# A spacer of 256 bytes between two generations of buffers in a hybrid decoder block

## The chip, the cores and the metric

The kernel is one launch on one core of a Trainium2 chip. The metric is the device time of that launch in microseconds (us). Of the kernel before, three timed runs are known (1938.85, 1940.31 and 1944.94 us; the median is 1940.31 us) and one profiled execution, whose trace is read here.

## The reference, cut to what matters

One layer of a decoder block, on a sequence of 2048 rows of width 1024, all in float32:

```
h = x + concat[RMSNorm(PoolMix(u)), RMSNorm(StickBreakAttn(q, k, v))] @ w_out
        with [u | q | k | v] = RMSNorm(x) @ w_in
up  = RMSNorm(h) @ w_up            # 1024 -> 4096
act = square(relu(up))
h   = h + act @ w_down             # 4096 -> 1024
y   = RMSNorm(h)
```

Only the last two products bear on this change. In the kernel the product with `w_up` is called layer one (function `up`) and the product with `w_down` layer two (function `down`).

## The kernel before, in words

Each float32 operand is split into two parts: a rounded copy that ScalarE writes (L146) and the remainder that VectorE writes (L147). A product is then three matmuls: high by high, high by low, low by high.

Both layers use Strassen's scheme: seven products P1 to P7 of half blocks, with sums made ahead on VectorE. Layer one runs over 16 columns of weights in two passes; each column is seven slots of 12 matmuls (L1052), accumulated in three PSUM banks named `pX`, `pY` and `pZ`. The split weights of a slot (`hw`) live in a ring of six buffers, the pool `hlp`. After a slot, `post` empties its bank: L987 copies it (`u`), L981 and L982 are relu and square, L997, L1005 and L1021 add a bank to an earlier copy, L1012, L1015, L1017 and L1025 form sums, L976 stores each result to DRAM (`sd`). For some results `inner_sums` makes more sums (L881, L883, L885, L887) and stores them (`sdi`, L879); its rows `hr` are read by L870. The last column's slots end with P7 and P4 (bank `pY`) and P3 (bank `pZ`). P3 goes on adding to the bank that L1005 reads first, and L1021 reads the finished P3.

Layer two starts with its product P1: eight steps `kk`, each of 48 matmuls (L1392), 24 for each half `q` of the rows. A step takes one block of weights (`wr`, loaded by L1121, 512 KB, split into `wd`), and two blocks of rows (`ar`, loaded by L1171 from layer one's results, 512 KB each, split into `ad`). It also takes a second weight block that L1125 subtracts from; the difference is stored (`td`, L1127). The rings are: `rt` with six buffers for `wr`, `rs` with five for `ar`, `t8` with three for `wd`, `s8` with five for `ad`. The residual rows `res` are read by L1196.

All these loads and stores are issued from SyncE's queue (SP), in order. Each uses one of eight semaphores in turn (DMAHW0 to DMAHW7), and waits until the transfer eight places ahead in the queue has landed.

Layer one's pools are closed before layer two's are opened, so the bytes are handed on. A buffer of layer two that shares even one byte with a buffer of layer one waits for the last reader of that buffer. The order of the instructions on each engine is not written by hand: a planner sets it when the kernel is built, from a model of when each instruction could run, and a wait of that kind goes into its model.

The pool `rs` begins where `pupa`, which holds 2 x 8192 bytes, ends: at byte 44,224 of each partition. Layer one's ring `hlp` ends at byte 44,288. The buffer of `hlp` that lies there, bytes 40,192 to 44,287, holds the split weights of layer one's very last slot, P3 of the last column.

Of the kernel before, what the change touches and what calls it, by code (L numbers as in the profile page):

```python
# [8 lines left out]
F32 = mybir.dt.float32  # L9
# [6 lines left out]
P = 128  # L16
# [24 lines left out]
DA = 2  # L41
# [5 lines left out]
def hymba_block(ctx: ExitStack, tc: tile.TileContext, xT, gains, w_in, pool_w, w_out, w_up, w_down, out):  # L47
# [1378 lines left out]
    def catch_up(n):  # L1426
        for _ in range(n):
            with ExitStack() as behind:
                for ins in (last_split[0], done[0]):
                    if ins:  # L1430
                        behind.enter_context(tc.issue_after(ins.ins))
                later.pop(0)()
# [42 lines left out]
    def ffn():  # L1475
        catch_up(len(later))
        front_scope.close()
        for _ in layer.pop():
            pass
        left_scope.close()  # L1480
        with ExitStack() as scope:
            spool = lambda name, bufs, **kw: scope.enter_context(tc.tile_pool(name=name, bufs=bufs, reuse_waits="tile", **kw))

            rlp, pupa, rs, rt, t8 = spool("rlp", 2), spool("pupa", 2), spool("rs", 5), spool("rt", 6), spool("t8", DA + 1)
            s8, tmp2, pup, rsp = spool("s8", 2 * DA + 1), spool("tmp2", 2), spool("pup", 6), spool("rsp", 2)
            down([t8, s8, rs, rt, pupa, pup, rsp, rlp, tmp2, spool("psb", 1, space=PS)])

# [21 lines left out]
    tail(True)  # L1509
    run()  # L1510
    ffn()


    count = P * H * (TB * NT - 2)
    got = nc.values_load(zeros[0:1, 0:1], min_val=0, max_val=count)
    with tc.If(got < count):
        wlist.clear(), raws.clear(), grans.clear(), gates.clear(), marks.clear()
        state["gran"], last_split[0], last_mm[0], done[:] = 0, None, None, (None, None)
        open_pools(front_scope)
        open_big(left_scope)  # L1520
        open_att(att_scope)
        for j in range(NT):
            far(j)
        att_scope.close()
        open_last(front_scope, last_scope)
        open_out(out_scope)
        tail(False)
        run()
        ffn()
# [44 lines left out]
```

## Time and profile before

| | us |
|---|---|
| median of the three runs | 1940.31 |
| the profiled execution's own time | 1938.94 |
| its span in the trace | 1937.1 |
| TensorE matmuls, busy | 1902.7 |
| VectorE, busy | 1383.2 |
| ScalarE, busy | 991.2 |

PE is TensorE's matmuls, PEld its weight loads, DVE is VectorE, ACT is ScalarE, POOL is GpSimd, SP is SyncE, and SPq is SyncE's queue that issues transfers. The granted clock (PEclk) is the share of its full speed at which TensorE was allowed to run. A row of the timeline gives a start, a length, the engine, the line, the operation with output and input, a count, and in brackets the idle time just before and what ended it.

### The profile page before, as it was taken

The numbers are of one execution on the slowest core, as the hardware profiler recorded it, in microseconds if no ns is written. First come the engines' busy times: TensorE is split into PE (matmuls) and PEld (weight loads), VectorE is DVE, ScalarE is ACT, GpSimd is POOL, SyncE is SP. The second block draws the span as 40 slices with busy tenths as digits, with TensorE's granted clock in tenths as the row PEclk, the third lists the DMA queues.
The fourth block names the chain that finished last, engine by engine and source line by source line (L and its number), as shares of the span: only waits on it lengthen the run. The fifth ranks groups of instructions, "written<-read, shape, count | busy, mean of one in ns | idle before, by whom it ended". The sixth has DMA issues, their size and how long they took to land.

```text
span 1937.1 us, 26281 instructions
## 1 busy us (share of the span) xinstructions
PE 1902.7 (98%) x9043; PEld 1588.3 (82%) x9043; DVE 1383.2 (71%) x2026; ACT 991.2 (51%) x1580; POOL 210.2 (11%) x399
## 2 busy tenths in 40 slices
PE   9999999999999999999999999997999999999997
PEld 7888888888888888888888888886888888887887
DVE  6887799668876975767587677774565558649874
ACT  5565566455544555555575555552333255425643
POOL 0211123102111110000000000000020020006120
PEclk9999999999999999999999999998999999999999
DMA  6686686888696964677476666579798869958852
GB/s 214 205 269 190 214 283 211 269 307 289 235 382 227 327 198 156 209 248 247 170 251 230 227 211 238 206 278 366 257 324 291 275 247 323 332 191 275 316 206 89
DMA packets 197359, 483.44 MB, mean 250 GB/s; under 512 B 22496, under 2 KB 42976, under 8 KB 193120
## 3 DMA queue, kind: packets, MB, share of 16 engines
q1 hardware_dynamic: 197072, 481.40, 72.2%
q8 instruction: 73, 1.20, 0.3%
q14 instruction: 70, 0.57, 0.1%
q10 hardware_dynamic: 144, 0.26, 0.0%
HBM read 320.10 MB, written 161.48 MB: 249 GB/s over the span
## 4 chain that ended last, share of the span: by engine, by line
PE 84%; issue 8%; DVE 4%; DMA 2%; POOL 1%; ACT 1%; SPq 0%; DVEq 0%; ACTq 0%; POOLq 0%
PE pY L1052 17%; PE pb L1392 17%; PE pZ L1052 8%; PE pd L175 8%; PE pd L177 8%; PE pd L176 8%; PE pX L1052 4%; PE pb L1230 2%; PE po L672 2%; PE pta L661 1%; PE pr L228 1%; PE pz L614 1%; PE pm L202 1%; DMA res<-hs 1%; PE pz L615 1%
## 5 line engine op out<-in xcount | busy, mean ns | idle before, releaser
L1392 PE MATMUL pb<-ad,wd 128*128 128x512 f32 x1872 | 429.8, 392 | 12.5 <-ACT ad L146 12.5
L1392 PEld LDWEIGHTS pb<-ad,wd 128*128 128x128 f32 x1872 | 352.9, 189 | 85.9 <-ACT ad L146 12.9
L1052 PE MATMUL pY<-sa,hw 128*128 128x512 f32 x1536 | 364.3, 390 | 1.2 <-ACT u L987 1.2
L1052 PEld LDWEIGHTS pY<-sa,hw 128*128 128x128 f32 x1536 | 288.2, 188 | 61.6 <-ACT u L987 2.0
L175 PE MATMUL pd<-h,hl 128*128 128x512 f32 x752 | 299.4, 398 | 0.7 <-DVE qkr L421 0.7
L177 PE MATMUL pd<-h,hl 128*128 128x512 f32 x752 | 296.6, 394 | 0.0
L176 PE MATMUL pd<-h,hl 128*128 128x512 f32 x752 | 296.5, 394 | 0.0
L146 ACT ACTIVATE ad<-ar 128x1024 fp32r<-128x1024 f32 x136 | 143.0, 1053 | 117.6 <-PE pb L1392 70.1
L147 DVE TENSOR_TENSOR ad<-ar,ad 128x1024 fp32r<-128x1024 f32 x136 | 175.2, 1298 | 32.6 <-ACT ad L146 32.5
L1052 PE MATMUL pZ<-sa,hw 128*128 128x512 f32 x768 | 184.7, 390 | 0.0
L1052 PEld LDWEIGHTS pZ<-sa,hw 128*128 128x128 f32 x768 | 144.2, 188 | 29.8
L175 PEld LDWEIGHTS pd<-h,hl 128*128 128x128 f32 x752 | 141.9, 189 | 28.0 <-DVE qkr L421 1.0
L177 PEld LDWEIGHTS pd<-h,hl 128*128 128x128 f32 x752 | 141.6, 188 | 27.7
L176 PEld LDWEIGHTS pd<-h,hl 128*128 128x128 f32 x752 | 141.7, 188 | 26.8
L146 ACT ACTIVATE hl<-raw 128x512 fp32r<-128x512 f32 x168 | 103.7, 630 | 108.2 <-PE pd L177 70.7
L1230 PE MATMUL pb<-ad,wd 128*128 128x512 f32 x672 | 153.9, 390 | 2.5 <-DVE ad L147 2.4
L1230 PEld LDWEIGHTS pb<-ad,wd 128*128 128x128 f32 x672 | 125.8, 188 | 30.3 <-DVE ad L147 4.4
L147 DVE TENSOR_TENSOR hl<-raw,hl 128x512 fp32r<-128x512 f32 x168 | 114.3, 687 | 49.4 <-ACT hl L146 48.9
L147 DVE TENSOR_TENSOR hw<-rt,hw 128x512 fp32r<-128x512 f32 x128 | 87.7, 688 | 56.8 <-ACT hw L146 55.9
L146 ACT ACTIVATE wd<-wr 128x1024 fp32r<-128x1024 f32 x48 | 50.7, 1061 | 148.7 <-PE pb L1392 126.5
L147 DVE TENSOR_TENSOR wd<-wr,wd 128x1024 fp32r<-128x1024 f32 x48 | 58.6, 1222 | 52.9 <-ACT wd L146 52.8
L1052 PE MATMUL pX<-sa,hw 128*128 128x512 f32 x384 | 93.1, 390 | 0.0
(213 smaller groups left out, 2632.2 us busy)
## 6 DMA issues: line engine op xcount, KB each, us to landing
ar<-sd SPq DMA_DIRECT2D x104, 512.0 KB, 5.7
rb<-in_w_up_dram SPq DMA_DIRECT2D x32, 1024.0 KB, 6.1
wr<-in_w_down_dram SPq DMA_DIRECT2D x64, 512.0 KB, 5.3
sd<-a SPq DMA_DIRECT2D x112, 256.0 KB, 3.3
raw<-in_w_in_dram SPq DMA_DIRECT2D x50, 512.0 KB, 4.9
sd<-s SPq DMA_DIRECT2D x96, 256.0 KB, 3.7
raw<-in_w_out_dram SPq DMA_DIRECT2D x32, 512.0 KB, 5.6
ar<-sdi SPq DMA_DIRECT2D x32, 512.0 KB, 5.5
```

What stands on the lines that cost most here:

```text
L146: nc.scalar.activation(hi, src, AF.Copy)
L147: return nc.vector.tensor_tensor(lo, src, hi.bitcast(F32), ALU.subtract)
L175: nc.tensor.matmul(ps, hl[:, 0, c], hi, start=(k == 0), stop=False)
L176: nc.tensor.matmul(ps, hl[:, 0, c], lo, start=False, stop=False)
L177: mm = nc.tensor.matmul(ps, hl[:, 1, c], hi, start=False, stop=(k == n - 1))
L202: marks["pm"] = nc.tensor.matmul(pm[:, c:c + 1], ss[:, c * P:(c + 1) * P], inv[n], start=(i == 0), stop=(i == len(parts) - 1))
L228: mm = nc.tensor.matmul(pr[:, b * P:(b + 1) * P], yr[:, x, b:b + 1].to_broadcast([P, P]), identr, start=(b == 0 and x == 0), stop=(b == TB ...
L614: nc.tensor.matmul(pz, qa[:, qsl], k, start=first, stop=False, skip_group_check=not (first and last))
L672: nc.tensor.matmul(po[:, p * 256 + to:p * 256 + to + hi - lo], vw[:, 2 * p + v], at[:, x, lo:hi], start=(p == 0 and n == 0 and x == 0), sk ...
L1052: nc.tensor.matmul(t, w[:, wx, c], a[:, ax, c % 2], start=first and c == 0 and x == 0, stop=last and c == G - 1 and x == 2, skip_group_che ...
L1230: nc.tensor.matmul(b, t[:, wx, 2 * (kk % 2) + c, i * P:(i + 1) * P], a[:, ax, c], start=p in ("P1", "P5", "P2") and kk == 0 and c == 0 and ...
L1392: nc.tensor.matmul(ps[q, n], t[:, wx, c, n * P:(n + 1) * P], left_[q][:, ax, c], start=(n_ in ("P1", "P5", "P3") and kk == 0 and c == 0 an ...
```

## The change

A pool named `even` is opened between `pupa` and `rs`. It holds one tile of 64 float32 in each partition, 256 bytes, that nothing writes or reads. All pools opened after it lie 256 bytes higher. The ring `rs` now begins at byte 44,480, past the end of `hlp` at 44,288; its first buffer shares bytes only with `rba`, layer one's ring for raw weights.

```
-            rlp, pupa, rs, rt, t8 = spool("rlp", 2), spool("pupa", 2), spool("rs", 5), spool("rt", 6), spool("t8", DA + 1)
+            rlp, pupa = spool("rlp", 2), spool("pupa", 2)
+            spool("even", 1).tile([P, 2 * P // 4], F32, name="even")
+            rs, rt, t8 = spool("rs", 5), spool("rt", 6), spool("t8", DA + 1)
             s8, tmp2, pup, rsp = spool("s8", 2 * DA + 1), spool("tmp2", 2), spool("pup", 6), spool("rsp", 2)
```

The planner's order differs only where layer one goes over into layer two; ahead of it all engines have the same order as before, and so they have again from the first steps of layer two's second product on. Three places are shown. Numbers behind a name tell buffers apart, and "waits" names the semaphores an instruction waits for.

On SP before, the first two loads of rows stand among the stores of layer one's last results, and the first waits for TensorE (PE_49):

```order
L1121 DMA wr_13564<-in_w_down_dram 128x1024 [waits DMAHW3_49]
L879 DMA sdi2_1_3_448<-j2_13262 128x512 [waits DMAHW4_49,DVE_49]
L879 DMA sdi2_2_3_452<-hr_13132 128x512 [waits DMAHW5_49,DVE_49]
L1171 DMA ar_13371<-sd0_0_0_313 128x1024 [waits DMAHW6_49,PE_49]
L879 DMA sdi2_3_3_456<-hr_13133 128x512 [waits DMAHW7_49,DVE_49]
L976 DMA sd1_3_7_400<-s1_13286 128x512 [waits DMAHW0_49,DVE_49]
L1171 DMA ar_13372<-sd1_0_0_369 128x1024 [waits DMAHW1_49]
```

On SP now, at a place that before held the two `hr` loads and then six loads of `wr` in a row:

```order
L976 DMA sd1_0_3_372<-a11_13050 128x512 [waits DMAHW2_49,Activation_49]
L1171 DMA ar_13375<-sd0_0_0_313 128x1024 [waits DMAHW3_49]
L870 DMA hr_13132<-sd0_2_3_332 128x512 [waits DMAHW4_49]
L870 DMA hr_13133<-sd0_2_7_336 128x512 [waits DMAHW5_49]
L1171 DMA ar_13376<-sd1_0_0_369 128x1024 [waits DMAHW6_49]
L1171 DMA ar_13394<-sd0_0_1_314 128x1024 [waits DMAHW7_49]
L1121 DMA wr_13373<-in_w_down_dram 128x1024 [waits DMAHW0_49,PE_49]
L1121 DMA wr_13388<-in_w_down_dram 128x1024 [waits DMAHW1_49,PE_49]
L1121 DMA wr_13392<-in_w_down_dram 128x1024 [waits DMAHW2_49]
L1171 DMA ar_13395<-sd1_0_1_370 128x1024 [waits DMAHW3_49]
L1121 DMA wr_13407<-in_w_down_dram 128x1024 [waits DMAHW4_49]
L1121 DMA wr_13411<-in_w_down_dram 128x1024 [waits DMAHW5_49]
```

The first load of rows stands 27 places further ahead, directly behind the store of `a11_13050`, and no longer waits for TensorE. A fifth load of rows and a sixth of `wr` follow. Three loads of rows now stand ahead of the first `wr`, four ahead of the fourth, five ahead of the sixth.

On ACT, at the end of layer one, before:

```order
L981 ACTIVATE a21_13283<-pY_13117 128x512 [waits DMAHW4_49,DMAHW2_49,PE_49]
L982 ACTIVATE a21_13283<-a21_13283 128x512 [waits Activation_49]
L981 ACTIVATE a12_13306<-a12_13306 128x512 [waits DVE_49]
L982 ACTIVATE a12_13306<-a12_13306 128x512 [waits Activation_49]
L146 ACTIVATE ad_13378<-ar_13371 128x1024 [waits DMAHW6_49]
L146 ACTIVATE ad_13381<-ar_13372 128x1024 [waits DMAHW1_49,PE_49]
```

and now:

```order
L981 ACTIVATE a21_13283<-pY_13117 128x512 [waits DMAHW1_49,PE_49]
L982 ACTIVATE a21_13283<-a21_13283 128x512 [waits Activation_49]
L981 ACTIVATE a12_13306<-a12_13306 128x512 [waits DMAHW5_49,DVE_49]
L146 ACTIVATE ad_13382<-ar_13375 128x1024 [waits DMAHW3_49]
L146 ACTIVATE ad_13385<-ar_13376 128x1024 [waits DMAHW6_49,PE_49]
L146 ACTIVATE ad_13401<-ar_13394 128x1024 [waits DMAHW7_49]
```

The five first splits of rows moved ahead by one place, past the last L982, but still stand behind the last L981, which works on what L1021 wrote. The tile `a12_13306` now lies in the buffer of `s4_13181`, so its writers wait for that tile's store (DMAHW5).

On DVE, some 10 instructions ahead of that L1021, before:

```order
L1125 TENSOR_TENSOR wr_13369<-wr_13384,wr_13369 128x1024 [waits DMAHW6_49,DVE_49]
L147 TENSOR_TENSOR wd_13413<-wr_13407,wd_13413 128x1024 [waits DMAHW1_49,Activation_49]
L1125 TENSOR_TENSOR wr_13388<-wr_13403,wr_13388 128x1024 [waits DMAHW0_49,DVE_49]
L1005 TENSOR_TENSOR a22_13256<-pZ_13229,u3_13254 128x512 [waits Activation_49]
L1125 TENSOR_TENSOR wr_13407<-wr_13422,wr_13407 128x1024 [waits DMAHW2_49,DVE_49]
L881 TENSOR_TENSOR j1_13261<-a22_13105,a22_13256 128x512 [waits Activation_49]
```

and now:

```order
L1125 TENSOR_TENSOR wr_13373<-wr_13388,wr_13373 128x1024 [waits DMAHW1_49,DVE_49]
L1125 TENSOR_TENSOR wr_13392<-wr_13407,wr_13392 128x1024 [waits DMAHW4_49,DVE_49]
L1005 TENSOR_TENSOR a22_13256<-pZ_13229,u3_13254 128x512 [waits Activation_49]
L147 TENSOR_TENSOR wd_13417<-wr_13411,wd_13417 128x1024 [waits DMAHW5_49,Activation_49]
L881 TENSOR_TENSOR j1_13261<-a22_13105,a22_13256 128x512 [waits Activation_49]
L1125 TENSOR_TENSOR wr_13411<-wr_13426,wr_13411 128x1024 [waits DMAHW7_49,DVE_49]
```

The same six instructions stand there; the split of `wd` and the third L1125 went behind L1005 and L881. Further on, the five L147 for `ad` stand directly behind L1021 now, ahead of the last five sums of layer one; before they stood behind those.

## The prediction

> **What bounds the kernel now.** I read the page first. Its row of busy times and the costliest group of layer two:
>
> ```profile
> span 1937.1 us, 26281 instructions
> PE 1902.7 (98%) x9043; PEld 1588.3 (82%) x9043; DVE 1383.2 (71%) x2026; ACT 991.2 (51%) x1580; POOL 210.2 (11%) x399
> L1392 PE MATMUL pb<-ad,wd 128*128 128x512 f32 x1872 | 429.8, 392 | 12.5 <-ACT ad L146 12.5
> ```
>
> TensorE is busy for all but 1937.1 - 1902.7 = 34.4 us, so the change can only pay, or cost, through TensorE's waits. The view of who waited for whom (total, times, longest) gives them for PE; its two largest rows are:
>
> ```profile
> PE pb L1392 <- ACT ad L146: 12.5, 1, 12.5
> PE pb L1230 <- DVE ad L147: 2.4, 3, 1.3
> ```
>
> A single wait of 12.5 us, before layer two's first product, is over a third of all idle time. The timeline of PE places it, the last row being PE in a narrower stretch:
>
> ```profile
> 1304.64 2.88 PE L1052 MATMUL pZ<-sa,hw 128*128 128x512 f32 x12
> 1320.05 25.28 PE L1392 MATMUL pb<-ad,wd 128*128 128x512 f32 x99 [12.52 <-ACT ad L146]
> ```
>
> Layer one's last slot, P3, ends at 1304.64 + 2.88 = 1307.52, and layer two starts at 1320.05. Next, the chain that ended last (start, length, what) through that wait:
>
> ```profile
> 1311.93 0.02 issue
> 1311.95 0.02 SPq L1171
> 1311.97 0.03 issue
> 1312.00 6.92 DMA ar<-sd
> 1318.92 0.02 issue
> 1318.94 1.06 ACT ad L146
> 1320.01 0.04 issue
> 1320.05 10.09 PE pb L1392 x32
> ```
>
> The first rows `ar` are asked for at 1312.00, land at 1318.92 and are split by 1320.00; TensorE starts with the split. So the load of the rows is late, no engine is.
>
> **The late load.** In the order of before it waits for TensorE, since its buffer shares 64 bytes with the weights of P3, which ends at 1307.52. It also stands in SP's queue behind layer one's last stores. The order now has it behind the store of `a11_13050`, which SP's timeline shows at 1284.19, without a wait for TensorE:
>
> ```profile
> 1284.19 0.40 SPq L976 DMA_DIRECT2D sd<-a  x1
> 1284.64 0.95 SPq L870 DMA_DIRECT2D hr<-sd  x2
> 1285.69 3.65 SPq L1121 DMA_DIRECT2D wr<-in_w_down_dram  x6
> 1312.00 0.32 SPq L1171 DMA_DIRECT2D ar<-sd  x1
> ```
>
> That is 27 us earlier, and even with the longest landing of a weight block there (9.8 us, below) rows are in place long before P3 ends.
>
> **What is late next.** The first split of rows stands on ACT behind the last L981, and that behind L1021 on DVE. The timelines of DVE and ACT for the stretch:
>
> ```profile
> 1297.51 2.36 DVE L147 TENSOR_TENSOR wd<-wr,wd 128x1024 fp32r<-128x1024 f32 x2 [0.21 <-ACT wd L146]
> 1299.79 1.22 DVE L1125 TENSOR_TENSOR wr<-wr 128x1024 f32<-128x1024 f32 x1
> 1303.19 0.69 DVE L1005 TENSOR_TENSOR a<-pZ,u 128x512 f32<-128x512 f32 x1
> 1303.79 1.22 DVE L1125 TENSOR_TENSOR wr<-wr 128x1024 f32<-128x1024 f32 x1
> 1305.24 0.69 DVE L881 TENSOR_TENSOR j<-a,a 128x512 f32<-128x512 f32 x1 [0.23 <-ACT a L982]
> 1309.84 0.68 DVE L1021 TENSOR_TENSOR a<-pZ,u 128x512 f32<-128x512 f32 x1
> 1296.43 2.94 ACT L146 ACTIVATE wd<-wr 128x1024 fp32r<-128x1024 f32 x3
> 1310.55 0.63 ACT L981 ACTIVATE a<-a 128x512 f32<-128x512 f32 x1 [4.19 <-DVE a L1021]
> ```
>
> From 1297.51 on DVE works almost without a gap until L1021 ends at 1310.52. The order now has the same instructions between, some swapped. So L1021 ends near 1310.5 again, if no operand is late. L981 then takes 0.63 (to 1311.18) and the first split 1.06 (the chain), and TensorE starts at about 1312.2: 7.8 us earlier than 1320.05. The swaps could save at most the 0.23 us in which DVE waited ahead of L881. The other four splits follow about 1 us apart (2.94 for three `wd` of the same size) and feed TensorE's next matmuls in time.
>
> **What the earlier loads push back.** Five loads of 512 KB now stand among the six of `wr`. The latter's rows in the view of L1121 for that stretch (issue length, first and last issue; time to landing), and the rate of all transfers in two slices (the last two columns are the transfer engines' share and GB/s):
>
> ```profile
> L1121 SPq DMA_DIRECT2D wr<-in_w_down_dram x6: 366/422/1113, 1285.7 to 1288.2; - x6
> DMA to landing us min/median/max: 6.0/8.0/9.8
> 1294.00:1295.00 1.00, 1.00 (x6) 0.84 (x5) 0.64 (x2) 0.33 (x1) 0.00 (x0) 1.00 1.04 426
> 1309.00:1310.00 1.00, 0.00 (x0) 0.00 (x0) 1.00 (x3) 0.00 (x0) 0.00 (x0) 1.00 0.96 252
> ```
>
> They land from 1291.7 to 1298.0, one every 6.3 / 5 = 1.27 us, with the transfer engines full. An estimate from that: each load of rows ahead of a block costs it 1.27 us. The first `wr` lands at 1291.7 + 3 x 1.27 = 1295.5 (its split on ACT starts at 1296.43), the third at 1298.0 against a second split at about 1297.4, the fourth at 1300.6 (its L1125 at about 1300.9), the fifth at 1301.9 (its split, now behind the copy for P4, at about 1301.8), the sixth at 1304.4 (its L1125 now behind L881, which was at 1305.24). So they arrive just in time, at worst 0.6 us late. Behind them, the store of `s4_13181`, whose buffer L1021 now waits for, can only be issued when the fifth block has landed at 1301.9, eight places ahead. Two blocks (2.54 us) and seven transfers of 256 KB, its own among them, must pass: 0.64 us each at the full rate, 1.0 us each at the 252 GB/s of the second slice where stores mix in. It lands between 1308.9 and 1311.4, against L1021 at 1309.84. I take 0.5 us for all this, near the lower end, since most rows of the stretch run at the higher rate; the upper end is 1.6 us, and the end on the other side is the 0.23 us above. If all five loads stood in the way at once it would be 5 x 1.27 = 6.35 us; that is the far bound.
>
> The Trainium skill's page "DMA: Bandwidth & Descriptors", section "Where 436 GB/s comes from", speaks against the change: it says that transfers between HBM and SBUF are bound at about 358 GB/s for a core. By that a block would take 1.46 us, an estimate, and five loads would cost 7.3 us. The slice with 426 GB/s above does not agree, and the measurement decides.
>
> **Where nothing is given back.** Once layer two runs, its steps of 48 matmuls need new rows. TensorE's pace is that of a row of 12 matmuls of the chain, and the first splits that had to wait are in the timelines:
>
> ```profile
> 1287.51 2.73 PE pY L1052 x12
> 1335.45 1.06 ACT L146 ACTIVATE ad<-ar 128x1024 fp32r<-128x1024 f32 x1 [0.58 <-DMA ar<-sd]
> 1337.30 2.36 DVE L147 TENSOR_TENSOR ad<-ar,ad 128x1024 fp32r<-128x1024 f32 x2
> ```
>
> Half a step is 24 matmuls, 5.45 us. The sixth split of rows, ready at about 1338.5, is used by the second half of step two, five halves in: 1320.05 + 5 x 5.45 = 1347.3. That is 8.8 us to spare, and 11.5 with the slow clock below. So 7.3 us of lead are covered even if that load came no earlier; but its place in SP's queue is now behind eight transfers fewer. Later waits (2.4 us at L1230) move with TensorE.
>
> **The sum.** 7.8 - 0.5 = 7.3 us off the profiled execution's 1938.94 us: **1931.6 us**. That execution is 1.4 us below the median of the three runs, 1940.31.
>
> **The clock.** The rows of the stretch by slices of 1 us (the third column from the right is the granted clock):
>
> ```profile
> 1310.00:1311.00 1.00, 0.00 (x0) 0.00 (x0) 0.52 (x1) 0.45 (x1) 0.00 (x0) 1.00 0.97 356
> 1311.00:1312.00 1.00, 0.00 (x0) 0.00 (x0) 0.12 (x1) 0.81 (x2) 0.00 (x0) 0.91 1.05 426
> 1312.00:1313.00 1.00, 0.00 (x0) 0.00 (x0) 0.57 (x1) 0.00 (x0) 0.00 (x0) 0.50 1.02 395
> 1324.00:1325.00 1.00, 1.00 (x4) 0.75 (x3) 0.34 (x1) 0.72 (x1) 0.00 (x0) 0.50 1.03 414
> 1325.00:1326.00 1.00, 1.00 (x5) 0.81 (x4) 0.63 (x1) 0.80 (x2) 0.00 (x0) 0.77 1.02 404
> ```
>
> The clock falls to half at about 1311.8, 4.3 us after TensorE stopped, and is back at about 1325.5, 5.4 us after it started. The 99 matmuls from 1320.05 therefore took 25.28 us where 99 x 2.73 / 12 = 22.5 would do: the wait costs another 2.7 us. The new wait would be 12.5 - 7.3 = 5.2 us. By these rows that is still longer than 4.3 us, so the forecast lets the clock fall and changes nothing in the 2.7 us.
>
> **The rivals.**
>
> *The clock holds.* If the fall came 0.9 us later than in this trace, a wait of 5.2 us would end before it, and the 2.7 us go too: 1931.6 - 2.7 = 1928.9 us. For it speaks that the wait is only just long enough; against it the one fall in the trace. The Trainium skill's page "TensorE: Matmul & The Clock Gate", section "Part 1: The HAM clock gate (the "warmup" mystery)", says that activity is judged in free-running windows of about 3.4 us, and that an idle one halves the clock. By that rule the outcome hangs on where the windows lie: a wait of 5.2 us need hold a whole window only in about half the executions, an estimate. The trace's fall after 4.3 us agrees with it but cannot show the other case.
>
> *The weight blocks or the store come late.* DVE works in order, so a late block holds L1125, and behind it L1005 (for which P3 waits) and L1021. With delays of 2 to 6.35 us the gain is 5.8 to 1.5 us: 1933.1 to 1937.4 us. For it speaks how narrowly the blocks arrive in the estimate above.
>
> *The same, past the break-even.* The earlier loads cost more than the late one did if L1021 ends later than 1310.52 + 7.8 = 1318.3, 7.8 us late. All five loads in the way give 6.35, so it needs these and another 1.5 us, say from each transfer waiting for the one eight places ahead. At 14 us late it would be 1938.94 + 6 = 1945 us. Against it: the transfer engines are full either way, and the same bytes are moved.
>
> *The change does nothing.* The ring `rs` still shares bytes with `rba`. But the first load no longer names TensorE, and SP reaches it 27 places earlier; so this can hardly be: 1939 to 1940 us.
>
> **How the numbers follow.** Forecast, clock falls: 0.46. Clock holds: 0.31. Blocks or store late: 0.14. Past the break-even: 0.05. Nothing: 0.04. The range, 1927.5 to 1936.5 us, reaches from the clock holding with a little less wait (1928.9 less the 0.5 and the 0.23, and rounding) to late blocks with 2.4 us of gain, and holds the first two cases with the 1.4 us to the median added. What a measurement of this kernel can tell from no change is about 0.3%, 5.8 us: faster means below 1934.5. The first two cases and a fifth of the third give faster 0.80; the rest of the third, the last and a little of the break-even case give same 0.16; slower 0.04.
>
> **What would show it.** Right: SP issues L1171 near 1285; PE's wait at L1392 is 4.3 to 6.5 us and still put down to ACT; L1021 on DVE ends between 1310 and 1312.5; TensorE's waits after that are as before. The slices behind P3 show whether the clock fell. Wrong: PE waits at L1052 for L1005 or L987, DVE waits for `wr` ahead of L1125, or L1021 waits for a store, each by more than 2 us; or a new wait at L1392 in the steps after.

## The result, and the profile after

The changed kernel took 1934.1 us (median of 13 runs, 1930.2 to 1940.3) against 1940.9 us for the kernel before (13 runs on the same chip): a ratio of 0.9965, 95% interval 0.9953 to 0.9977, or 6.8 us less. Run once more among the experiments it took 1936.2 us, a ratio of 0.9976 (0.9966 to 0.9987), 5.0 us below the 1941.27 us of before beside it. So it is faster, by 0.2 to 0.4%. The profiled execution took 1934.94 us.

Busy times and the costliest group on the page of the changed kernel, which answer to 1902.7 busy and 12.5 us of waiting before:

```profile
span 1933.1 us, 26290 instructions
PE 1902.3 (98%) x9043; PEld 1586.1 (82%) x9043; DVE 1384.3 (72%) x2026; ACT 991.0 (51%) x1580; POOL 205.8 (11%) x399
L1392 PE MATMUL pb<-ad,wd 128*128 128x512 f32 x1872 | 429.6, 391 | 4.8 <-ACT ad L146 4.8
```

The work is the same to 0.4 us. What changed is the wait. Who waited for whom, on PE (total, times, longest):

```profile
PE pb L1392 <- ACT ad L146: 4.8, 1, 4.8
PE pb L1230 <- DVE ad L147: 3.8, 4, 1.3
```

12.5 us at L1392 became 4.8, still one wait, still put down to the split of rows, but the reason has changed. The chain that ended last, of the changed kernel (start, length, what):

```profile
1287.15 0.45 SPq L1171
...
1292.97 11.62 DMA wr<-in_w_down_dram
...
1304.61 1.07 ACT wd L146
...
1312.58 0.61 DVE a L1021
...
1313.21 0.03 ACT a L981
1313.24 0.51 issue
1313.75 1.05 ACT ad L146
1314.80 0.04 issue
1314.84 15.29 PE pb L1392 x56
```

Before, the piece ahead of the split was `DMA ar<-sd`, 6.92 us. The load of rows is now issued at 1287.15, and what ends last is L1021, L981, split: layer one's own last results. ScalarE's timeline of before shows how long the first split stood for the load alone:

```profile
1311.21 0.63 ACT L982 ACTIVATE a<-a 128x512 f32<-128x512 f32 x1
1318.94 1.06 ACT L146 ACTIVATE ad<-ar 128x1024 fp32r<-128x1024 f32 x1 [7.10 <-DMA ar<-sd]
```

These 7.10 us are gone. So is the L982 of 0.63 us, past which the planner moved the split in the same step; together they make up the 7.7 us by which the wait fell. PE's timeline gives the length of the pause:

```profile
1307.15 2.88 PE L1052 MATMUL pZ<-sa,hw 128*128 128x512 f32 x12
1314.84 30.48 PE L1392 MATMUL pb<-ad,wd 128*128 128x512 f32 x123 [4.81 <-ACT ad L146]
```

P3 ended at 1310.03, 2.5 us later than in the profile of before. TensorE's wait in this stretch is the same 0.69 us in both, so that is taken as scatter between executions: in the profiles below that leave the alignment of layer one's split weights alone, P3 ends anywhere from 1305.78 to 1312.12, with early and late loads mixed. A measure without it is the time from the end of P3 to the end of the span: 1937.1 - 1307.52 = 629.6 us before, 1933.1 - 1310.03 = 623.1 us after. It is used below and called **the tail**.

### The profile page after: what moved, and what is told of

It is laid out like the page before. It is cut to its first block, busy times and chain, and to the rows that moved or that the text cites. A ratio compares the mean times of both kernels' runs of the same rounds, so it can differ in the third digit from the quotient of the medians.

```text
span 1933.1 us, 26290 instructions
## 1 busy us (share of the span) xinstructions
PE 1902.3 (98%) x9043; PEld 1586.1 (82%) x9043; DVE 1384.3 (72%) x2026; ACT 991.0 (51%) x1580; POOL 205.8 (11%) x399
## 4 chain that ended last, share of the span: by engine, by line
PE 88%; DVE 6%; DMA 4%; issue 1%; ACT 1%; POOL 0%; SPq 0%; DVEq 0%; ACTq 0%
PE pb L1392 21%; PE pY L1052 17%; PE pZ L1052 8%; PE pd L175 7%; PE pd L177 7%; PE pd L176 7%; PE pb L1230 6%; PE pX L1052 4%; PE po L672 2%; PE pta L661 1%; PE pr L228 1%; PE pz L614 1%; PE pz L615 1%; PE pm L202 1%; DMA raw<-in_w_in_dram 1%
## 5 line engine op out<-in xcount | busy, mean ns | idle before, releaser
L1392 PE MATMUL pb<-ad,wd 128*128 128x512 f32 x1872 | 429.6, 391 | 4.8 <-ACT ad L146 4.8
L1392 PEld LDWEIGHTS pb<-ad,wd 128*128 128x128 f32 x1872 | 352.4, 189 | 78.4 <-ACT ad L146 5.2
L1052 PE MATMUL pY<-sa,hw 128*128 128x512 f32 x1536 | 364.2, 389 | 1.8 <-ACT u L987 1.8
L1052 PEld LDWEIGHTS pY<-sa,hw 128*128 128x128 f32 x1536 | 288.2, 188 | 62.3 <-ACT u L987 2.7
L147 DVE TENSOR_TENSOR ad<-ar,ad 128x1024 fp32r<-128x1024 f32 x136 | 173.3, 1286 | 34.2 <-ACT ad L146 34.2
L1052 PE MATMUL pZ<-sa,hw 128*128 128x512 f32 x768 | 184.6, 389 | 0.0
L1052 PEld LDWEIGHTS pZ<-sa,hw 128*128 128x128 f32 x768 | 144.1, 188 | 29.9
L1230 PE MATMUL pb<-ad,wd 128*128 128x512 f32 x672 | 154.1, 390 | 3.8 <-DVE ad L147 3.8
L1230 PEld LDWEIGHTS pb<-ad,wd 128*128 128x128 f32 x672 | 125.6, 188 | 32.0 <-DVE ad L147 6.1
L147 DVE TENSOR_TENSOR hl<-raw,hl 128x512 fp32r<-128x512 f32 x168 | 114.4, 687 | 51.2 <-ACT hl L146 48.0
L147 DVE TENSOR_TENSOR hw<-rt,hw 128x512 fp32r<-128x512 f32 x128 | 87.6, 688 | 56.6 <-ACT hw L146 55.8
L147 DVE TENSOR_TENSOR wd<-wr,wd 128x1024 fp32r<-128x1024 f32 x48 | 58.6, 1222 | 60.2 <-ACT wd L146 60.0
L1052 PE MATMUL pX<-sa,hw 128*128 128x512 f32 x384 | 93.1, 389 | 0.0
```

What stands on the lines that cost most here:

```text
L147: return nc.vector.tensor_tensor(lo, src, hi.bitcast(F32), ALU.subtract)
L1052: nc.tensor.matmul(t, w[:, wx, c], a[:, ax, c % 2], start=first and c == 0 and x == 0, stop=last and c == G - 1 and x == 2, skip_group_che ...
L1230: nc.tensor.matmul(b, t[:, wx, 2 * (kk % 2) + c, i * P:(i + 1) * P], a[:, ax, c], start=p in ("P1", "P5", "P2") and kk == 0 and c == 0 and ...
L1392: nc.tensor.matmul(ps[q, n], t[:, wx, c, n * P:(n + 1) * P], left_[q][:, ax, c], start=(n_ in ("P1", "P5", "P3") and kk == 0 and c == 0 an ...
```

## The experiments

Each ratio is against the kernel before, measured beside it. A diff is against the changed kernel unless it says otherwise. The tail and the wait come from one profiled execution of each kernel.

### 256 bytes behind the ring of rows

```
+            rs = spool("rs", 5)
             spool("even", 1).tile([P, 2 * P // 4], F32, name="even")
-            rs, rt, t8 = spool("rs", 5), spool("rt", 6), spool("t8", DA + 1)
+            rt, t8 = spool("rt", 6), spool("t8", DA + 1)
```

> The same 256 bytes are put behind the ring for rows (rs) instead of ahead of it: rs stays at byte 44,224 and keeps its 64 bytes in common with layer one's ring of split weights, while every buffer behind rs moves by 256 bytes as in the changed kernel. The order of the instructions around the start of layer two is that of before (first load of rows behind the sum stores, in row 1023 of SP, waiting for TensorE). If the gain is the early loads (theory), this is as slow as before: 1940.9 us, within 1.5, with some 12.5 us of waiting at L1392. If it is the new addresses of the buffers behind rs, or only how this launch fell (rivals), it is near the changed kernel: 1934 us.

Measured: 1940.35 us, ratio 0.999 (0.998 to 0.9999). PE's timeline, span 1937.9 us:

```profile
1305.76 2.88 PE L1052 MATMUL pZ<-sa,hw 128*128 128x512 f32 x12
1320.35 4.92 PE L1392 MATMUL pb<-ad,wd 128*128 128x512 f32 x13 [11.71 <-ACT ad L146]
```

Tail 1937.9 - 1308.64 = 629.3 us. Time, wait and tail are those of before to within 0.2%, 0.8 and 0.3 us: moving the other buffers is not the cause.

### The bytes shared again

```
-        rtp, hlp, rba, srp = (spool(n, b) for n, b in (("rtp", 1), ("hlp", UA + 2), ("rba", 1), ("srp", SR)))
+        rtp = spool("rtp", 1)
+        spool("odd", 1).tile([P, 2 * P // 4], F32, name="odd")
+        hlp, rba, srp = (spool(n, b) for n, b in (("hlp", UA + 2), ("rba", 1), ("srp", SR)))
```

> The changed kernel with 256 more bytes ahead of layer one's ring of split weights, so that its last buffer ends at 44,544 and shares 64 bytes with rs (44,480) again: every address of layer two is that of the changed kernel. The order is that of before (first load in row 1023). Theory (the shared ring puts the loads late, whatever the addresses): 1940.9 us within 1.5, wait at L1392 11.5 to 12.6 us. Rival (the addresses carry the gain): 1934 us.

Measured: 1942.55 us, ratio 1.0003 (0.9993 to 1.0014); the profiled span is 1942.9 us.

```profile
1309.24 2.88 PE L1052 MATMUL pZ<-sa,hw 128*128 128x512 f32 x12
1323.96 1.65 PE L1392 MATMUL pb<-ad,wd 128*128 128x512 f32 x3 [11.83 <-ACT ad L146]
```

Tail 630.8 us. With every address of layer two as in the changed kernel, pushing layer one's ring (and the rings behind it) up until it lies on `rs` again takes the whole gain away.

### 64 bytes: no split weights shared, the load still late

```
-            spool("even", 1).tile([P, 2 * P // 4], F32, name="even")
+            spool("even", 1).tile([P, 16], F32, name="even")
```

> A pool of 64 bytes instead of 256: rs starts at 44,288, exactly where layer one's last buffer of split weights ends, so no byte is shared. The load's wait for TensorE is gone, but its place in SP's queue is still row 1023, as before. The theory that the place in the queue carries the gain: the load can only move up to the row ahead of it, which before issued at 1310.07 us against 1312.00 for the load, so at most 1.6 us: 1939.3 to 1941 us, and a wait at L1392 of 11 to 12.5 us. The rival that the 64 bytes and the wait made by them carry it: 1934 us, wait near 5 us.

Measured: 1941.65 us, with 1942.41 us for the kernel before beside it, ratio 0.9997 (0.9988 to 1.0006), span 1940.3 us. PE's timeline, then SP's:

```profile
1307.25 2.88 PE L1052 MATMUL pZ<-sa,hw 128*128 128x512 f32 x12
1321.85 3.35 PE L1392 MATMUL pb<-ad,wd 128*128 128x512 f32 x7 [11.72 <-ACT ad L146]
```
```profile
1311.68 0.70 SPq L879 DMA_DIRECT2D sdi<-hr  x1
1313.70 0.32 SPq L1171 DMA_DIRECT2D ar<-sd  x1
```

No gain, although `rs` shares no byte with the split weights and the load names TensorE no more. It issues 1313.70 - 1310.13 = 3.6 us after P3, against 4.5 before (1312.00 - 1307.52) and 3.7 in the kernel with the 256 bytes behind the ring, where the load does name TensorE. So the wait for TensorE was not what held it: its place in SP's queue did.

What decides the place shows in the planner's order for other sizes, of which only 64, 224 and 256 bytes were timed. With pools of 64, 96, 128 or 192 bytes the load is in row 1023, with 224 in row 989, with 256 or 512 in row 996. The limit is byte 44,448, where layer one's next buffer (`rba`) begins: between it and the end of the split weights at 44,288 lie 160 bytes that belong to `hlp` only because its buffers are placed on multiples of 256. So it seems that the planner keeps the loads back as long as `rs` lies on that padding too; the kernel without padding, below, tries it.

### 224 bytes: still earlier

```
-            spool("even", 1).tile([P, 2 * P // 4], F32, name="even")
+            spool("even", 1).tile([P, 56], F32, name="even")
```

> A pool of 224 bytes: rs starts at 44,448, where layer one's next ring (the rows' buffer behind the split weights) starts. The five loads are put still earlier in SP's queue (rows 989 on against 996 on), one of them with a wait for VectorE; the splits stay behind the last two activations of layer one. Theory (loads are ready long before the splits can run; the split waits for L981 and that for L1021): nothing more to gain, 1934 us within 1.5, wait at L1392 4.5 to 5.3 us. Rival (the landing of the loads still counts): 1 to 2 us faster, 1932 to 1933. Rival (earlier loads push back layer one's stores and weights, as the late wr and s loads of the changed kernel already show): 1935 to 1937.

Measured: 1933.58 us, ratio 0.9958 (0.9944 to 0.9971), span 1927.1 us:

```profile
1302.90 2.88 PE L1052 MATMUL pZ<-sa,hw 128*128 128x512 f32 x12
1310.60 14.68 PE L1392 MATMUL pb<-ad,wd 128*128 128x512 f32 x57 [4.82 <-ACT ad L146]
```

The wait is that of the changed kernel to 0.01 us although the first load is issued at 1278.76, 8.4 us earlier: landing no longer counts. Tail 621.3 us, 1.8 less than in the changed kernel; the clock, which came back 3.1 us after the restart instead of 4.9 (last section), accounts for part of it. By the medians it is not told from the changed kernel.

### No padding at all

```
-            hl = hlp.tile([P, 2, G, P], F32R, tag="hw", name="hw", align_bytes=256)
+            hl = hlp.tile([P, 2, G, P], F32R, tag="hw", name="hw")
```

(The diff is against the kernel before.)

> The kernel before, without any pool, but with layer one's split weights no longer placed on multiples of 256 bytes: their ring then ends at 44,224, exactly where rs starts, with no padding behind it. The loads of rows stand in rows 989 on of SP, as with the pool of 224 bytes. Theory (the loads were late because rs lay on the last 64 bytes and on the 160 bytes of padding of that ring, and on nothing else): 1934 us within 2, from the end of P3 to the end of the span 621 to 623.5 us, against 629 to 631 in the kernels with late loads. Rival (the alignment matters to TensorE's reads of the weights): layer one slower, well above 1941 us.

Measured: 1940.75 us, ratio 0.9999 (0.9986 to 1.0012), span 1936.7 us: no gain in all. The theory holds for the transition, the rival for layer one. PE's timeline, and the group of L1052 in layer one, in this kernel:

```profile
1311.94 2.91 PE L1052 MATMUL pZ<-sa,hw 128*128 128x512 f32 x12
1319.62 10.65 PE L1392 MATMUL pb<-ad,wd 128*128 128x512 f32 x39 [4.77 <-ACT ad L146]
```
```profile
L1052 PE MATMUL pY<-sa,hw x1536: 387/392/503, 694.0 to 1311.7; 128*128 128x512 f32 x192
```

and that group in the changed kernel (duration in ns: least, median, most; first and last start):

```profile
L1052 PE MATMUL pY<-sa,hw x1536: 388/389/500, 695.4 to 1306.9; 128*128 128x512 f32 x192
```

The tail is 1936.7 - 1314.85 = 621.9 us, with a wait of 4.77: the transition has the whole gain, without any pool. But layer one ran from 694.0 to 1311.7, 617.7 us against 611.5, and its matmuls are longer, with a median of 392 against 389 ns. In the other twelve profiles the same rows give 610.1 to 612.6 us and 389 or 390 ns, so this is more than scatter. What the transition gains, layer one gives back.

### The changed kernel again, and the pause filled

> The changed kernel once more, unedited, as the yardstick of this call and as a second draw of the clock: 1934 us within 1.5, wait at L1392 4.8 us within 0.3. If the clock's fall depends on where the pause lies against some free count of time, its fall after P3 and its return after the restart differ by some tenths to 3 us from the first profile (2.9 and 4.8 us); if it is a fixed delay, they repeat.

Measured: 1936.23 us, 0.7 us above what was expected; span 1930.1 us:

```profile
1303.92 2.88 PE L1052 MATMUL pZ<-sa,hw 128*128 128x512 f32 x12
1311.34 14.02 PE L1392 MATMUL pb<-ad,wd 128*128 128x512 f32 x50 [4.53 <-ACT ad L146]
```

Tail 623.3 us, as the first time. The clock fell at 1309.68 and was back at 1316.52, 2.9 us after P3 and 5.2 us after the restart, against 2.9 and 4.9 us in the first profile. This pair alone does not tell a free count of time from a fixed delay; the other kernels do (last section). Measured beside it, with extra matmuls in the pause:

```
+        wb = bank(0)
+        for _ in range(40):
+            nc.tensor.matmul(wb[:, 0:2 * P], identb, maskb.rearrange("p i n -> p (i n)"), start=True, stop=True)
```

> The changed kernel with 40 extra matmuls of 128x256 between P3 and layer two's first matmul, which write a bank that is overwritten afterwards; they fill the pause of 4.8 us and do nothing else. Theory (the clock falls because TensorE stands idle, and that costs by itself): the pause is as long, the clock stays at 1.0, and 2.4 us go: 1931.7 us, within 1.5. Rival (the clock's fall costs nothing net, since VectorE and the transfers set the pace of the first groups): 1934 us. Rival (the extra matmuls run past the pause): slower by what they overrun, up to 2 us, 1936.

Measured: 1933.82 us, ratio 0.996 (0.9947 to 0.9973), span 1932.0 us. PE's timeline, and a slice where the clock of the changed kernel is at half (length, PE busy, granted clock, the transfer engines' share, GB/s):

```profile
1307.45 2.88 PE L1052 MATMUL pZ<-sa,hw 128*128 128x512 f32 x12
1310.17 4.54 PE L1375 MATMUL pb<-maskb,identb 128*128 128x256 bf16 x40
1314.86 0.50 PE L1395 MATMUL pb<-ad,wd 128*128 128x512 f32 x1
1316.12 9.18 PE L1395 MATMUL pb<-ad,wd 128*128 128x512 f32 x39 [0.76 <-DVE ad L147]
```
```profile
1316.00:1317.00 1.00, 0.88 (x4) 1.00 1.07 410
```

The pause is as long, and the clock holds. The tail is 1932.0 - 1310.33 = 621.7 us: 1.5 us are saved, not 2.4 (half of the 4.9 us from 1314.84 to 1319.74 that the changed kernel ran at half clock). At full speed TensorE reaches the low half of the first split before VectorE has made it, and waits 0.76 us; with the slow clock that wait was hidden. The order of the first matmuls also differs a little. The median missed the 1930.2 to 1933.2 us of the theory, though the changed kernel beside it was above its own expectation too, at 1936.2. The medians (0.996 against 0.9976, intervals that overlap) agree with a small saving but show no more.

### One split ahead of L981

```
-                split((left_[q][:, 0], left_[q][:, 1]), rows[q])
+                with tc.high_priority() if g == 0 and q == 0 else nullcontext():
+                    split((left_[q][:, 0], left_[q][:, 1]), rows[q])
```

> The changed kernel with the first split row of layer two alone put ahead of the last L981 on ScalarE; VectorE's half of that split stays behind L1021, and ScalarE's L981 stays behind L1021 for the other splits. Theory (the pause is the chain L1021, L981, first split): TensorE gets four matmuls right behind P3, then waits for VectorE's half, which is done some 2.3 us after L1021's start instead of 2.9: waits of about 1.3 to 3 us in all in place of 4.8, in two pieces too short for the clock to fall: 1930 to 1932 us. Rival (VectorE's half sets the end as before, and the four matmuls only move forward): 1933 to 1934.5 us.

Measured: 1933.78 us, ratio 0.9958 (0.9944 to 0.9973), span 1928.0 us. PE's timeline, and slices as above:

```profile
1304.32 2.88 PE L1052 MATMUL pZ<-sa,hw 128*128 128x512 f32 x12
1308.03 1.21 PE L1393 MATMUL pb<-ad,wd 128*128 128x512 f32 x4 [0.83 <-ACT ad L146]
1311.26 13.91 PE L1393 MATMUL pb<-ad,wd 128*128 128x512 f32 x53 [2.01 <-DVE ad L147]
```
```profile
1312.00:1313.00 1.00, 1.00 (x4) 0.57 1.05 408
1315.00:1316.00 1.00, 1.00 (x5) 0.72 1.04 424
```

The pause is 0.83 + 2.01 = 2.84 us instead of 4.8, so the chain of L1021, L981 and split did set it; what is left ends with VectorE's half of the split, which still stands behind L1021. The tail is 1928.0 - 1307.20 = 620.8 us, 2.4 less than in the changed kernel. The median is above the 1930 to 1932 of the theory and in the rival's range, but not precise enough to decide. The clock fell all the same, at 1312.1, against what the theory expected.

### Two rings for the split rows

In the changed kernel the second split row lies on bytes 147,200 to 155,391. Layer one's activations for P3's last six matmuls end at 147,968, and the copy `u2_13224` that L1021 reads lies at 154,112. That is another shared edge, on the other operand.

```
-            s8, tmp2, pup, rsp = spool("s8", 2 * DA + 1), spool("tmp2", 2), spool("pup", 6), spool("rsp", 2)
+            s8 = [spool("s8a", 2), spool("s8b", 2 * DA - 1)]
+            tmp2, pup, rsp = spool("tmp2", 2), spool("pup", 6), spool("rsp", 2)
...
+        def ad_tile():
+            k = turn_of[0] % (2 * DA + 1)
+            turn_of[0] += 1
+            return s8[k > 1].tile([P, 2, 2, T], F32R, tag="ad", name="ad", align_bytes=256)
```

(The two places that took a tile from `s8` call `ad_tile()` now.)

> The changed kernel with the ring of five split-row buffers (s8) cut in two pools of two and three, taken in turn, so that the first two split rows lie on memory that layer one frees early. Both splits then stand ahead of L982 of the block before the last on ScalarE, and ahead of L1005 of it on VectorE, and TensorE's first twelve groups of L1392 need no wait on ScalarE behind P3. Theory (what is left of the gap is the chain P3, L1021, L981, split): TensorE goes on without a pause, 4.8 us of waiting and the 2.4 us of the fallen clock go, less up to 2.3 us for two splits on VectorE (2 x 1.15) and 1.9 on ScalarE inside layer one: 1927 to 1930 us, clock 1.0 throughout. Rival (the wait only moves, to the third split, which still stands behind L981 and L1021, or into layer one): 1932 to 1935 us.

Measured: 1926.0 us, ratio 0.992 (0.9907 to 0.9934), span 1923.6 us. PE's timeline, then VectorE's:

```profile
1302.40 3.02 PE L1052 MATMUL pY<-sa,hw 128*128 128x512 f32 x12 [0.79 <-ACT u L987]
1305.57 3.04 PE L1052 MATMUL pZ<-sa,hw 128*128 128x512 f32 x12 [0.16 <-DVE a L1005]
1308.45 16.94 PE L1398 MATMUL pb<-ad,wd 128*128 128x512 f32 x74
```
```profile
1301.42 1.22 DVE L147 TENSOR_TENSOR ad<-ar,ad 128x1024 fp32r<-128x1024 f32 x1
...
1303.70 1.22 DVE L147 TENSOR_TENSOR ad<-ar,ad 128x1024 fp32r<-128x1024 f32 x1
```

TensorE goes on without a pause, and the median is 1 us below what was expected. The two splits lie in layer one, and TensorE's waits there grow from 0.69 to 0.79 + 0.16 us, not by the 2.3 us allowed for. The tail is 1923.6 - 1308.61 = 615.0 us, 8.1 below the changed kernel. Of that, 4.8 is the wait and some 2.4 the slow clock (the estimate of above); 0.9 was not placed.

> The kernel with two rings once more, unedited: 1926 us within 1.5, 615 us within 0.5 from the end of P3 to the end of the span, no wait at the first L1398.

Measured: 1929.29 us, ratio 0.9938 (0.9919 to 0.9958). The wait was again absent and the clock full; P3 ended at 1309.29 and the span at 1924.9, a tail of 615.6 us. The median missed what was expected. In both runs the kernel is faster than both others: 0.9920 and 0.9938 of before, where the changed kernel had 0.9965 and 0.9976.

### The two rings alone

The kernel above without the pool `even`.

> The two rings for split rows (as in the kernel with two rings) without the pool of 256 bytes: rs is at 44,224 again. The first load of rows stands in row 1023 of SP, as before; the split rows' buffers are free early, as in the kernel with two rings. Theory (the late loads bind as long as they are late, and the two rings only pay behind early loads): as before, 1941 us within 2, wait at L1392 11 to 12.6 us. Rival (the two rings carry their gain alone): 1932 to 1934 us.

Measured: 1941.13 us, ratio 1.0 (0.9988 to 1.0011), span 1938.6 us.

```profile
1305.57 2.88 PE L1052 MATMUL pZ<-sa,hw 128*128 128x512 f32 x12
1320.16 10.11 PE L1398 MATMUL pb<-ad,wd 128*128 128x512 f32 x32 [11.71 <-ACT ad L146]
```

Tail 630.2 us. Free buffers for the splits are worth nothing as long as the loads are late: the two edits do not add, the second works only behind the first.

## Why the prediction was right, point by point

| | late loads | early loads |
|---|---|---|
| kernels | before; 256 behind; shared again; 64 bytes; rings alone | changed, twice; 224 bytes; no padding |
| wait at the first matmul of layer two, us | 12.5; 11.7; 11.8; 11.7; 11.7 | 4.8; 4.5; 4.8; 4.8 |
| tail, us | 629.6; 629.3; 630.8; 630.2; 630.2 | 623.1; 623.3; 621.3; 621.9 |

The five late tails have a mean of 630.0, the changed kernel's two 623.2: the change is worth 6.8 us at its place. The prediction's 7.3 is near. The changed kernel's median lay 2.5 us above the forecast of 1931.6, most of it because the sum started from one execution of 1938.94 us and the runs of before had a median of 1940.9. The medians alone bear the forecast out narrowly: 1934.1 us is just below the 1934.5 that the prediction asked of a faster kernel, and the 1936.2 of the second measurement is above it. The tails are what settles it.

*The late load.* Right in its effect: issued at 1287.15 and out of the chain. Of its two reasons one falls. The prediction named the wait for TensorE that the 64 shared bytes make, and the place in SP's queue; the kernel with 64 bytes shares no byte with the split weights and has no such wait, and is as slow as before. The place is what counts, and the padding holds it back as well as the bytes. In every kernel with early loads the planner also put the splits ahead of the last L982; by the rows of ScalarE above that is worth about 0.6 us of the wait, and the load the rest. That the bytes set the place, as the description of the kernel has it, is thus only part of it.

*What is late next.* L1021, then L981, then the split, as predicted. From the start of L1021 to TensorE's start it is 1314.84 - 1312.49 = 2.35 us, and from the end of P3 to that L1021 2.46. These 2.46 us are no wait for an operand: VectorE works through the sums that stand ahead of L1021 without a gap. So what is left of the pause hangs on the place of L1021 in VectorE's order, which no run here tests by itself. Some rows of VectorE's timeline, then of ScalarE's:

```profile
1305.70 1.23 DVE L147 TENSOR_TENSOR wd<-wr,wd 128x1024 fp32r<-128x1024 f32 x1 [0.46 <-ACT wd L146]
1312.49 0.69 DVE L1021 TENSOR_TENSOR a<-pZ,u 128x512 f32<-128x512 f32 x1
```
```profile
1304.61 1.06 ACT L146 ACTIVATE wd<-wr 128x1024 fp32r<-128x1024 f32 x1 [0.37 <-DMA wr<-in_w_down_dram]
1308.50 0.60 ACT L981 ACTIVATE a<-pY 128x512 f32<-128x512 f32 x1 [1.65 <-DMA sd<-s]
```

*What the earlier loads push back.* Before, L1021 started 1309.84 - 1307.52 = 2.32 us after P3; now 2.46. So the allowance of 0.5 us measured 0.14. Over all profiles with a pause, L1021 starts 2.30 to 2.32 us after P3 with late loads and 2.19 to 2.47 with early ones, so the cost lies within 0.2 us of nothing. The fifth block of weights came about when it was estimated: it landed at 1304.59 by the chain, where the estimate gives 1301.9 and this execution ran 2.5 us later. ACT waited 0.37 us for it and DVE 0.46 for ACT. The store was a miss: L1021 did not wait for that of `s4_13181`. ACT's L981 that reads `pY` waited 1.65 us for another store, which it did not before, but ACT was idle behind it anyway.

*The sum* is the step that was a little off: the wait fell by 12.52 - 4.81 = 7.7 us, not 7.3, but four other kernels with late loads wait only 11.7 to 11.8, so the profile of before lay high and 7.0 is nearer.

*Nothing given back* held: there is no second wait at L1392. L1230 shows 3.8 us where the profile of before had 2.4, but that is no price of the change: the late-load kernels with 64 bytes and with the bytes shared again have 3.5 and 4.6.

*The clock* fell, as forecast, and it did in all ten profiles of kernels with a pause that was not filled. The price was put at 2.7 us; filling the pause saved 1.5. But the reason for the forecast, that a pause of over 4.3 us is long enough, is not how it went: the fall came 2.9 us after P3 here, and between 2.8 and 5.1 in the others. So the outcome was right, and its reason was not. Nor was the prediction's estimate borne out that such a pause drops the clock in only about half the executions: all four profiles with a single pause of 4.5 to 4.8 us show the fall. The last section has a reading that fits: spread evenly over two windows of 3.41 us, a pause of 4.8 us still leaves each only about 30% busy, an estimate, and a window 41% busy was enough for a fall.

## What to carry to other kernels

When a stage begins with loads that stand late in a queue, look for whose bytes their buffers take over, padding included, and move the ring rather than the load: here 224 bytes were enough, and by the planned order 192 are not. Taking a semaphore off an instruction that a planner has already put late brings nothing; compare the order, not the waits. After such an edit read the chain again: the next edge was a ring for the other operand, worth another 8 us of the tail, and worth nothing without the first. Before removing a padding, see what it is for: taking it out cost 6 us elsewhere.

## What the runs showed of the hardware

In these profiles the granted clock steps on a grid of 3.41 us. The slices of the changed kernel at the fall and the return, and of the kernel with 224 bytes (columns as above):

```profile
1312.00:1313.00 1.00, 0.00 (x0) 0.96 0.93 381
...
1319.00:1320.00 1.00, 1.00 (x5) 0.63 1.01 408
```
```profile
1310.00:1311.00 1.00, 0.40 (x1) 0.64 1.03 395
1313.00:1314.00 1.00, 1.00 (x5) 0.65 1.00 408
```

A clock of 0.96 is half speed in 8% of the slice, so the first fell at 1312.92; 0.63 is 74%, so it came back at 1319.74: 6.82 us at half speed. In the other the same working gives 1310.28 to 1313.70, 3.42 us. The further stretches, read in the same way, are 3.41 and 3.42 (no padding; one split ahead), 6.84 (changed, again), 10.24 (256 behind) and four of 13.65 or 13.66 us: one, two, three and four times 3.41. The Trainium skill, page "TensorE: Matmul & The Clock Gate", section "Part 1: The HAM clock gate (the "warmup" mystery)", says that the clock follows activity in a window of about 3.4 us that runs free of the kernel. The traces agree: the lengths above are whole numbers of such windows, and the fall comes at no fixed time after TensorE stops (2.8 to 5.1 us).

What these runs add is that a window need not be wholly idle to drop the clock. If the windows end at these steps, the one before the fall at 1312.14 in the kernel with one split ahead began at 1308.73. By the rows shown there TensorE worked in it until 1309.24 (1308.03 + 1.21) and again from 1311.26: 0.51 + 0.88 = 1.39 us of 3.41, or 41% busy. The clock fell, with no pause over 2.01 us. In the kernel with 256 bytes behind, whose fall came at 1313.73, the window before the last ended at 1310.32 and was 51% busy, P3 ending at 1308.64; it did not drop the clock. On the way back, a window that was 68% busy (64 bytes, restart at 1321.85, window to 1324.17) did not restore it, and one that was 91% busy (224 bytes, restart at 1310.60, window to 1313.70) did. Whether these are fixed limits the runs do not show.

With the split weights at addresses 64 bytes short of a multiple of 256, the 2688 matmuls of layer one took some 2 to 3 ns longer each: 392 against 389 ns by the rows, and 6.2 us in all from the first start to the last. This is one offset and one profile. Layer one's other rings moved with the weights; the matmuls' other operand, `sa`, stayed on multiples of 256, so the address of the weights is the likely cause, but no run has it alone.
